# Low parts of the heads' weights: negated copy plus an accumulating DMA in place of a subtraction on VectorE

## The chip, the cores and the metric

The kernel runs on one core of a Trainium2 chip. A core has five engines that run beside each other, each with its own instruction queue that is worked off in order: TensorE (PE, matmuls; its weight loads are PEld), VectorE (DVE), ScalarE (ACT), GpSimd (POOL) and SyncE (SP, which here only issues DMAs). DMAs are issued from SP, ACT or POOL and run on 16 DMA engines. The metric is the device time of one execution in microseconds (us); a smaller one is better.

## The reference, cut to what matters

One decoder layer on a sequence of 512 tokens of width 2048, in float32. The input is normalised and multiplied by one wide matrix `w_in`; its columns feed 8 attention heads of width 128 (the "fox" heads, with a forget gate), 16 recurrent heads of width 64 (RWKV-7), and two gates.

```
h = rmsnorm(x, norm_gain)
u = h @ w_in                                   # 2048 x 12488 weights
u_fox, u_rwkv, g_a, g_b = split(u)
q, k, v, z_a, f = split(u_fox)                 # fox heads
o_a = fox_attention(q, k, v, logsigmoid(f + bias)) * silu(z_a)
r, kr, vr, z_b, w_down, a_down = split(token_shift(u_rwkv))
o_b = groupnorm(rwkv7_scan(r, decay, k, v, kk, b)) ... * silu(z_b)
m = sigmoid(g_a) * (o_a @ w_proj_fox) + sigmoid(g_b) * (o_b @ w_proj_rwkv)
out = rmsnorm(x + m @ w_out, final_norm_gain)
```

## The kernel before, in words

**Numbers as two parts.** TensorE multiplies in a rounded form of float32 (F32R). Each float32 operand is split in a high part (the rounded number) and a low part (what the rounding left), and a product is three matmuls: high x high, high x low, low x high. The normalised input lies in SBUF once as `hhi` and `hlo`. The weights come from HBM piece by piece (`load_raw`, tile `raw_*`), and `split_pieces` makes of each piece `whi_*` and `wlo_*`. From piece 4 on, ACT makes `whi` (L267, a Copy that rounds) and DVE makes `wlo` (L268, raw minus whi). `raw`, `whi` and `wlo` have four buffers each, so a piece takes over the buffers of the piece four before it.

**The heads stage** (about 40 to 930 us) takes 16 units in turn, RWKV pair 0, fox head 0, RWKV pair 1 and so on. Each unit has four tiles of 128 columns of `w_in` (k, r, z, v for an RWKV pair; fq, fk, fv, fz for a fox head), each tile four pieces of 512 weight rows (`HK` = 4 blocks of 128). So there are 64 tiles and 256 pieces of 128x512 (256 KB), and each piece feeds 12 matmuls of 512 columns into `u_*`. In the names `raw_fq_4` is the piece of tile fq that begins at block 4.

Beside the products, as generators that are stepped between matmuls, run the heads' own computations: `rwkv_front` (decay, normalised keys), `rwkv_back` (masked scores `G`, a triangular inverse `W` solved in 31 pairs of DVE instructions, L483 and L643), `rwkv_chain` and `fox_head` (logits, softmax, transposes). `rwkv_chain` goes through 8 chunks of 64 tokens one after the other; in each, PE makes `z`, which DVE and ACT copy to `zt` (L717, L718, half of the partitions each), PE makes `sa`, copied to `AV` (L727, L728), and PE makes `st`, added by DVE into the next state `SV` (L735). The ACT half of `zt` and of `AV` waits for the DVE half of the same tile.

**What sets the order.** PE and SP follow the order of the program text, which a small planner fixes: it counts matmul time in `clock` and resumes each generator after a delay from the table `LAG`. DVE, ACT and POOL are ordered by a scheduler that takes priorities: evictions of products and of the chain have `high_priority(offset=HP)`, HP = 300, the splitting of pieces has HW = 150. On POOL there is little in the heads stage: two elementwise instructions a pair (L533, L483), copies and clears for the chain (L708, L595), and the stores of the heads' results (L774 `ob_d`, L837 `oa_d`).

`next_piece`, called when PE comes to piece i, issues loads up to piece i + 4 and has the split of pieces up to i + 2 put into the program.

After the heads come the gates (from about 930 us; pieces g, then loads named `b` and `X`, where sums of `w_in` blocks are made, one of them by a DMA from POOL that adds into `X`, L985), the projections (p) and the output (o).

Of the kernel before, what the change touches and what calls it, by code (L numbers as in the profile page):

```python
# [9 lines left out]
F32 = mybir.dt.float32  # L10
F32R = mybir.dt.float32r
AF = mybir.ActivationFunctionType
ALU = mybir.AluOpType
# [43 lines left out]
def hybrid_layer(  # L57
# [7 lines left out]
    V, S, G, PE = nc.vector, nc.scalar, nc.gpsimd, nc.tensor  # L65
# [171 lines left out]
    def load_raw(name, srcs, nk, M):  # L237
        raw = wpool.tile([P, nk, M], F32, tag="raw", bufs=RAWS, name=f"raw_{name}")
        for off, src in srcs:
            nc.sync.dma_start(raw[:, :, off:off + src.shape[1]], src.rearrange("(k p) m -> p k m", p=P))  # L240
        return raw

    def next_piece():


        i = used[0]
        used[0] += 1
        while len(raws) < min(i + (RAWS + 1 if i > 3 else 4), len(pieces)):
            raws.append(load_raw(*pieces[len(raws)]))
        split_pieces(i + (3 if i > 3 else 1))  # L250
        got = parts[i]
        parts[i] = None
        return got

    def split_pieces(n):
        while len(parts) < min(n, len(pieces)):
            j = len(parts)
            name, srcs, nk, M = pieces[j]
            raw = raws[j]
            whi = wpool.tile([P, nk, M], F32R, tag="whi", bufs=4, name=f"whi_{name}")  # L260
            wlo = wpool.tile([P, nk, M], F32R, tag="wlo", bufs=4, name=f"wlo_{name}")
            if j < 4:
                G.tensor_copy(whi, raw)
                G.tensor_tensor(wlo, raw, whi.bitcast(F32), ALU.subtract)
            else:
                with tc.high_priority(offset=HW):
                    S.activation(whi, raw, AF.Copy)  # L267
                    V.tensor_tensor(wlo, raw, whi.bitcast(F32), ALU.subtract)  # L268
            parts.append((whi, wlo))


# [7 lines left out]
    def product(ps, name, hi, lo):  # L279

        M, nk = spec[name]
        for k0 in range(0, nk, HK):
            whi, wlo = next_piece()
            for k in range(HK):
                kk = k0 + k
                mm(ps[0:M, :], whi[:, k, :], hi(kk), start=(kk == 0), stop=False)
                yield
                mm(ps[0:M, :], whi[:, k, :], lo(kk), start=False, stop=False)
                yield
                mm(ps[0:M, :], wlo[:, k, :], hi(kk), start=False, stop=(kk == nk - 1))  # L290
                yield
# [52 lines left out]
    for hf in range(2):  # L344
        t = slice(256 * hf, 256 * hf + 256)
        for j in range(0, KC + AHEAD, 2):
            if j < KC:
                turn(hf, j)
            if hf == 0 and j % 4 == 0 and j < KC:
                wd_w.append(next_piece())  # L350
                if j == 0:
                    for tb in range(2, 4):
                        for h2 in range(2):
                            load_x(nc.sync, tb, h2)
                    load_params()
            if hf == 0 and j in (SQ2, SQ3):
                norm_rows(2 if j == SQ2 else 3)
            if j < AHEAD:
                continue
            for kk in range(j - AHEAD, j - AHEAD + 2):  # L360
                whi, wlo = wd_w[kk // 4]
                mm(ps_wd[0:MW, t], whi[:, kk % 4, :], hhi[:, kk, t], start=(kk == 0), stop=False)
                mm(ps_wd[0:MW, t], whi[:, kk % 4, :], hlo[:, kk, t], start=False, stop=False)
                mm(ps_wd[0:MW, t], wlo[:, kk % 4, :], hhi[:, kk, t], start=False, stop=(kk == KC - 1))
            if hf == 1 and j - AHEAD in (4, 8, 12):
                split_pieces(4 + (j - AHEAD) // 4)
# [492 lines left out]
    def stage1():  # L859
# [198 lines left out]
        for g in range(4):  # L1058
            ps = [ps_mm(f"c11_{g}_0"), (ps_mm if g else ps_y)(f"c11_{g}_1")]
            for kb in range(2):  # L1060
                for j in range(4):
                    ws = [next_piece(), next_piece()]
                    order = [(kk, t) for kk in range(2) for t in range(2)]
                    if j == 3:
                        order = [(kk, t) for t in range(2) for kk in range(2)]
                    for kk, t in order:
                        k = 2 * j + kk
                        ah, al = (a[:, KB * kb + k, t * P:(t + 1) * P] for a in (hhi, hlo))
                        whi, wlo = (w[:, 0, :] for w in ws[kk])
                        for a, w, i in ((ah, whi, 0), (ah, wlo, 1), (al, whi, 2)):  # L1070
                            mm(ps[t], a, w, start=kb == 0 and k == 0 and i == 0,
                               stop=kb == 1 and k == KB - 1 and i == 2, skip_group_check=True)
                            yield
                        if j == 3 and kk == 1:
                            if kb == 0:
                                p1 = keep.tile([P, T], F32, tag=KEEP[t], name=f"p1_{g}_{t}")
                                with tc.high_priority(offset=HP):
                                    S.copy(p1, ps[t])
                                    nc.scalar.dma_start(p1_d[g, t], p1)
                            else:  # L1080
                                sg = keep.tile([P, T], F32, tag=KEEP[2 + t], name=f"c11_{g}_{t}")
                                with tc.high_priority(offset=HP):
                                    S.activation(sg, ps[t], AF.Tanh, scale=0.5)
                                store_gate(sg, g, 0, 0, t)
                    if free["fox"] == 7 and first_sums:
                        sum_step(*first_sums.pop(0))
                    if g == 3 and kb == 1 and not first_sums:
                        sum_step("s2", j)
                    if g == 3 and kb == 1 and j == 3:
                        open_late()  # L1090
# [134 lines left out]
    for n in range(4):  # L1225
        pss = four_banks(n, f"o_{n}")
        for kk in range(KC if n < 3 else KC // 2):
            whi, wlo = next_piece()
# [61 lines left out]
```

## Time and profile before

| | |
|---|---|
| median of 3 runs (range) | 1658.53 us (1658.02 to 1660.35) |
| profiled execution: time | 1658.03 us |
| profiled execution: span of its instructions | 1656.3 us |
| PE busy | 1598.2 us, 96% of the span |
| DVE busy | 1125.3 us, 68% |
| ACT busy | 770.0 us, 46% |
| POOL busy | 103.4 us, 6% |
| mean granted TensorE clock | 0.994 of full speed |

Busy shares are means over the whole run. A PE that is busy may still not be at its peak, as matmuls overlap and their ends are modelled; an idle time of PE in the trace is time in which it had nothing to run. "PE sa L136 <- ACT zt L718: 5.1, 8" reads: PE stood idle 5.1 us in 8 places before a matmul into `sa`, until ACT's instruction of line 718 into `zt` was done.

### The profile page before, as it was taken

What the parts mean: (1) busy time and instruction counts of PE and PEld (TensorE: products, weight loads), DVE (VectorE), ACT (ScalarE), POOL (GpSimd) and SP (SyncE); (2) the same over time, 40 slices, a digit from 0 to 9 for tenths busy, and PEclk for the clock granted to TensorE, in tenths of its full rate; (3) what the DMA queues carried; (4) which work ended last, traced back from release to release, by engine and by line L of the source; (5) the groups of instructions that cost most, each with busy time, mean ns of one, the idle gap of its engine ahead of it and who ended that gap; (6) DMA issues with size and microseconds to landing.
All of it is one profiled execution on the core that took longest, in us unless ns stands there. A gap on an engine that the chain in (4) does not pass through costs nothing. (4 is left out here: it accounts for less than half of the span.)

```text
span 1656.3 us, 23493 instructions
## 1 busy us (share of the span) xinstructions
PE 1598.2 (96%) x8378; PEld 1297.9 (78%) x8378; DVE 1125.3 (68%) x2173; ACT 770.0 (46%) x1503; POOL 103.4 (6%) x165
## 2 busy tenths in 40 slices
PE   6999999999999999999999999799999999999998
PEld 6888787787787887878878777578878787888886
DVE  6468777786687687777866869997877335544432
ACT  7533645536436446455364467444444222323322
POOL 3010000000101000001000000011100000001110
PEclk9999999999999999999999999899999999999999
DMA  5443334243333342433333466878775545463422
GB/s 169 99 102 88 86 87 106 64 118 87 87 93 97 88 108 75 105 94 79 97 93 87 124 177 197 267 204 249 209 236 153 178 157 157 149 217 119 140 83 102
DMA packets 238315, 216.39 MB, mean 131 GB/s; under 512 B 40326, under 2 KB 174062, under 8 KB 237558
## 3 DMA queue, kind: packets, MB, share of 16 engines
q1 hardware_dynamic: 224582, 183.40, 39.3%
q0 software_dynamic: 6416, 17.85, 4.7%
q10 hardware_dynamic: 7200, 13.63, 2.2%
q8 instruction: 66, 1.08, 0.3%
q14 instruction: 51, 0.42, 0.1%
HBM read 193.84 MB, written 20.99 MB: 130 GB/s over the span
## 5 line engine op out<-in xcount | busy, mean ns | idle before, releaser
L136 PE MATMUL p<-whi_p,o 128*128 128x512 f32 x512 | 164.7, 398 | 2.2 <-ACT whi_p L267 2.2
L136 PEld LDWEIGHTS p<-whi_p,o 128*128 128x128 f32 x512 | 96.9, 189 | 24.6 <-ACT whi_p L267 3.0
L483 DVE TENSOR_TENSOR Wt<-W,Lt 128x16 f32<-128x16 f32 (+30 forms) x248 | 101.7, 410 | 6.4
L268 DVE TENSOR_TENSOR wlo_p<-raw_p,whi_p 128x512 fp32r<-128x512 f32 x64 | 43.5, 690 | 90.0 <-ACT whi_p L267 90.0
L136 PE MATMUL p<-wlo_p,o 128*128 128x512 f32 x256 | 101.2, 395 | 0.4 <-DVE wlo_p L268 0.4
L267 ACT ACTIVATE whi_p<-raw_p 128x512 fp32r<-128x512 f32 x64 | 40.4, 632 | 121.2 <-DMA raw_p<-in_w_proj_fox_dram 42.7
L268 DVE TENSOR_TENSOR wlo_o<-raw_o,whi_o 128x512 fp32r<-128x512 f32 x56 | 42.4, 761 | 74.9 <-ACT whi_o L267 74.7
L136 PE MATMUL o<-whi_o,mhi 128*128 128x512 f32 x224 | 87.6, 391 | 0.0
L136 PE MATMUL o<-whi_o,mlo 128*128 128x512 f32 x224 | 87.2, 389 | 0.0
L136 PE MATMUL o<-wlo_o,mhi 128*128 128x512 f32 x224 | 87.1, 389 | 0.0
L423 ACT CAST h<-X 128x1024 fp32r<-128x1024 f32 x48 | 50.2, 1052 | 66.9 <-DVE X L483 31.5
L643 DVE TENSOR_REDUCE W<-Wt 128x8 f32<-128x16 f32 (+30 forms) x248 | 72.7, 293 | 5.7
L267 ACT ACTIVATE whi_o<-raw_o 128x512 fp32r<-128x512 f32 x56 | 35.3, 631 | 83.8 <-PE o L136 75.9
L424 DVE TENSOR_TENSOR l<-X,h 128x1024 fp32r<-128x1024 f32 x48 | 58.3, 1222 | 19.2 <-ACT h L423 19.1
L136 PEld LDWEIGHTS p<-wlo_p,o 128*128 128x128 f32 x256 | 48.6, 190 | 11.8 <-DVE wlo_p L268 1.1
L722 ACT ACTIVATE pre<-SV,E 64x64 f32<-64x64 f32 x112 | 38.6, 345 | 39.5 <-DVE SV L735 38.3
L136 PE MATMUL c<-whi_g,hhi 128*128 128x512 f32 x128 | 51.6, 403 | 3.9 <-ACT whi_g L267 2.0
L423 ACT CAST h<-b 128x1024 fp32r<-128x1024 f32 x32 | 33.7, 1054 | 45.4 <-PE y L136 21.1
L136 PE MATMUL c<-wlo_g,hhi 128*128 128x512 f32 x128 | 51.3, 401 | 1.9 <-DVE wlo_g L268 1.9
L136 PE MATMUL u_fq<-hhi,whi_fq 128*128 128x512 f32 x128 | 52.5, 410 | 0.0
L136 PE MATMUL u_fq<-hlo,whi_fq 128*128 128x512 f32 x128 | 52.4, 409 | 0.0
L267 ACT ACTIVATE whi_g<-raw_g 128x512 fp32r<-128x512 f32 x64 | 39.8, 630 | 26.7 <-PE c L136 7.7
(423 smaller groups left out, 4663.9 us busy)
## 6 DMA issues: line engine op xcount, KB each, us to landing
b<-in_w_in_dram SPq DMA_DIRECT2D x64, 512.0 KB
raw_g<-in_w_in_dram SPq DMA_DIRECT2D x64, 256.0 KB
raw_o<-in_w_out_dram SPq DMA_DIRECT2D x56, 256.0 KB
raw_k<-in_w_in_dram SPq DMA_DIRECT2D x32, 256.0 KB
raw_r<-in_w_in_dram SPq DMA_DIRECT2D x32, 256.0 KB
raw_z<-in_w_in_dram SPq DMA_DIRECT2D x32, 256.0 KB
raw_v<-in_w_in_dram SPq DMA_DIRECT2D x32, 256.0 KB
raw_fq<-in_w_in_dram SPq DMA_DIRECT2D x32, 256.0 KB
```

Of the source, the lines that this page charges most:

```text
L136: PE.matmul(out, lhsT=lhsT, rhs=rhs, start=start, stop=stop, **kw)
L267: S.activation(whi, raw, AF.Copy)
L268: V.tensor_tensor(wlo, raw, whi.bitcast(F32), ALU.subtract)
L423: S.copy(hi, a)
L424: V.tensor_tensor(lo, a, hi.bitcast(F32), ALU.subtract)
L483: eng.tensor_tensor(o, a, b, op)
L643: V.tensor_reduce(W[:, :, i], tmp[:, :, 0:i + 1], AX.X, ALU.add)
L722: S.activation(pre[hs[q]], SV[hs[q], c, q, :], AF.Copy, scale=E1[hs[q], c, CH:CH + 1])
```

## The change

In `split_pieces`, pieces whose name begins with k, r, z, v or f (all 256 of the heads; not the first eight of the down projections and none of the gates, projections or output) no longer get their low part from DVE. ACT writes the negated, rounded raw piece into `wlo`, a DMA issued from POOL adds the raw piece onto it (SBUF to SBUF, `accum_op=ALU.add`), and ACT makes `whi` as before. In `next_piece` the splits are put into the program one piece further ahead (i + 4 in place of i + 3) for i from 8 to 249.

```diff
-        split_pieces(i + (3 if i > 3 else 1))
+        split_pieces(i + (4 if 7 < i < 250 else 3 if i > 3 else 1))
...
                 with tc.high_priority(offset=HW):
+                    if name[0] in "krzvf":
+
+                        S.activation(wlo, raw, AF.Copy, scale=-1.0)
+                        G.dma_start(wlo.bitcast(F32), raw, accum_op=ALU.add)
                     S.activation(whi, raw, AF.Copy)
-                    V.tensor_tensor(wlo, raw, whi.bitcast(F32), ALU.subtract)
+                    if name[0] not in "krzvf":
+                        V.tensor_tensor(wlo, raw, whi.bitcast(F32), ALU.subtract)
```

The order of PE and that of SP are the same before and after. On ACT 256 instructions come in, on POOL 256 DMAs, and on DVE 256 go; the scheduler also puts some of DVE's and ACT's other instructions of the heads stage in another order. From about 960 us on, ACT, DVE and POOL run the same rows in the same order.

ACT in the chain of the fourth pair (chunks 3 and 4), before; `zt` and `AV` are the copies that PE waits for, `pre` scales the state for the next chunk, `vT` is the eviction of tile v:

```order
L718 COPY zt_4261<-z_3_4259 64x64
L267 ACTIVATE whi_fq_4_4304<-raw_fq_4_4243 128x512
L728 COPY AV_4017<-sa_3_4274 64x64
L722 ACTIVATE pre_4316<-SV_3271,E_0_483 64x64 x2
L267 ACTIVATE whi_fq_8_4349<-raw_fq_8_4280 128x512
L718 COPY zt_4313<-z_4_4311 64x64
L267 ACTIVATE whi_fq_12_4371<-raw_fq_12_4302 128x512
L728 COPY AV_4017<-sa_4_4331 64x64
```

and after:

```order
L723 COPY zt_4378<-z_3_4376 64x64
L271 ACTIVATE whi_fq_4_4399<-raw_fq_4_4359 128x512
L269 ACTIVATE wlo_fq_4_4400<-raw_fq_4_4359 128x512
L733 COPY AV_4128<-sa_3_4391 64x64
L727 ACTIVATE pre_4435<-SV_3360,E_0_483 64x64 x2
L271 ACTIVATE whi_fq_8_4422<-raw_fq_8_4397 128x512
L269 ACTIVATE wlo_fq_8_4423<-raw_fq_8_4397 128x512
L723 COPY zt_4432<-z_4_4430 64x64
L271 ACTIVATE whi_fq_12_4468<-raw_fq_12_4420 128x512
L733 COPY AV_4128<-sa_4_4450 64x64
```

The same pieces stand at the same places of the chain, with the negating copy (L269) behind the rounding one, ahead of `AV` of chunk 3 and of `zt` of chunk 4.

POOL at the end of the fourth pair's chain, before (`SV` and `AV` belong to the next pair, `ob_d` stores a finished pair):

```order
L837 DMA oa_d<-fz_4345 128x512
L595 MEMSET SV_6698 64x64 x2
L708 COPY AV_6307<-SV_5537 64x8x64 x2
L774 DMA ob_d<-y_5858 128x512
L533 TENSOR_SCALAR a_6431<-a_6431 128x512
```

and after:

```order
L713 COPY AV_5352<-SV_4508 64x8x64 x2
L270 DMA wlo_fv_4_4803<-raw_fv_4_4666 128x512
L270 DMA wlo_fv_8_4840<-raw_fv_8_4800 128x512
L270 DMA wlo_fv_12_4862<-raw_fv_12_4837 128x512
L270 DMA wlo_fz_0_4881<-raw_fz_0_4859 128x512
L270 DMA wlo_fz_4_4900<-raw_fz_4_4878 128x512
L779 DMA ob_d<-y_4820 128x512
L270 DMA wlo_fz_8_4919<-raw_fz_8_4897 128x512
L270 DMA wlo_fz_12_4940<-raw_fz_12_4916 128x512
```

The accumulating DMAs stand in one queue with POOL's other work; the one of `fz_8` is behind the store `ob_d`, which waits for DVE.

## Rows read from the trace of the kernel before

**Rows 1.** Windows: busy us of each engine (instructions), clock, DMA share, GB/s; heads, gates.
```profile
100.00:930.00 830.00, 817.57 (x4771) 662.87 (x4770) 625.58 (x1431) 416.51 (x910) 42.94 (x56) 1.00 0.36 92
1150.00:1200.00 50.00, 50.00 (x220) 41.00 (x220) 41.37 (x41) 22.66 (x26) 3.69 (x4) 1.00 0.80 240
```

**Rows 2.** Windows: seven stretches in which a pair's front and chain begin, the first and the sum.
```profile
170.00:190.00 20.00, 17.20 (x136) 12.73 (x135) 15.58 (x26) 16.00 (x32) 2.38 (x2) 1.00 0.27 66
...
sum 220.00, PE 209.16 PEld 164.72 DVE 151.36 ACT 163.70 POOL 13.31; mean PE 29.88 PEld 23.53 DVE 21.62 ACT 23.39 POOL 1.90
```

**Rows 3.** Waits of PE, 100 to 930 us: us in total, times, longest.
```profile
PE sa L136 <- ACT zt L718: 5.1, 8, 1.5
PE z L136 <- ACT G L693: 1.7, 1, 1.7
PE bt L140 <- ACT BT L668: 1.1, 2, 0.8
```

**Rows 4.** Line 718 (ACT `zt`): what it waited for, who waited for it (us, times).
```profile
  DVE zt L717: 27.6, 31
...
  PEld sa L136: 12.1, 21
  PE sa L136: 5.1, 8
```

**Rows 5.** Waits of DVE, 100 to 930 us: us in total, times, longest.
```profile
DVE AV L727 <- PE sa L136: 16.6, 19, 2.3
DVE zt L717 <- PE z L136: 13.8, 13, 1.6
```

**Rows 6.** Groups of DVE in the same stretch: xcount, busy us, mean ns, idle before.
```profile
L717 DVE COPY zt<-z 64x64 f32<-64x64 f32 x56 | 11.9, 213 | 14.7 <-PE z L136 13.8
L727 DVE COPY AV<-sa 64x64 f32<-64x64 f32 x56 | 11.7, 209 | 16.8 <-PE sa L136 16.6
```

**Rows 7.** Window 100 to 930 us of line 268 alone: DVE busy (instructions).
```profile
100.00:930.00 830.00, 162.84 (x236) 1.00 0.36 92
```

**Rows 8.** Group of ACT, 100 to 930 us, one tile of eight like it.
```profile
L267 ACT ACTIVATE whi_fv<-raw_fv 128x512 fp32r<-128x512 f32 x32 | 20.2, 632 | 28.0 <-PE u_fk L136 27.1 <-DMA Lt<-l_d 0.7
```

**Rows 9.** POOL's queue (packets, MB, share); its DMA issues (count, KB, us to landing).
```profile
q0 software_dynamic: 6416, 17.85, 4.7%
...
X<-in_w_in_dram POOLq DMA_DIRECT2D x16, 512.0 KB, 7.2
...
oa_d<-fz POOLq DMA_DIRECT2D x8, 256.0 KB, 2.3
...
gain<-in_final_norm_gain_dram POOLq DMA_DIRECT2D x1, 1024.0 KB, 5.1
```

**Rows 10.** Timeline (start, us): a tight piece of tile r, twice.
```profile
495.48 0.62 ACT L267 ACTIVATE whi_r<-raw_r 128x512 fp32r<-128x512 f32 x1
...
499.08 0.39 PE L136 MATMUL u_r<-hhi,wlo_r 128*128 128x512 f32 x1
...
719.94 0.61 ACT L267 ACTIVATE whi_r<-raw_r 128x512 fp32r<-128x512 f32 x1
...
723.53 0.39 PE L136 MATMUL u_r<-hhi,wlo_r 128*128 128x512 f32 x1
```

**Rows 11.** Timeline: a low part, and the load that takes its raw buffer.
```profile
475.10 0.68 DVE L268 TENSOR_TENSOR wlo_k<-raw_k,whi_k 128x512 fp32r<-128x512 f32 x1
475.81 0.37 SPq L240 DMA_DIRECT2D raw_r<-in_w_in_dram  x1
```

**Rows 12.** Chain of waits: a raw load of 256 KB; twelve matmuls of 512 columns.
```profile
997.99 3.20 DMA raw_g<-in_w_in_dram
...
1063.42 2.75 PE x L136 x12
```

**Rows 13.** Timeline: a store on POOL, and PE at the piece queued behind it.
```profile
470.50 0.55 POOL L774 DMA_DIRECT2D ob_d<-y  x1 [18.30 <-DVE W L643]
...
476.12 0.39 PE L136 MATMUL u_fz<-hhi,wlo_fz 128*128 128x512 f32 x1
```

## The prediction, made before the changed kernel was run

> **What bounds the kernel now.** I read the windows by stage first. In the heads stage, the only one the change touches, PE is busy 817.6 of 830 us [rows 1], so 12.4 us of idle is all that a faster split can give back there, short of waits that overlapping matmuls hide. DVE is busy 625.6 us (75%) and ACT 416.5 (50%); neither is full on average, but averages hide the stretches. So second: seven stretches in which a pair's front and chain begin, together 220 us, hold 220 - 209.2 = 10.8 us of the 12.4 [rows 2]. There ACT is busy 163.7 us (74%) and DVE 151.4 (69%): ACT is the fuller engine exactly where PE idles. Third, the waits of PE: the largest is `sa` after ACT's `zt`, 5.1 us, and the next ones are ACT's too [rows 3]. Fourth, who was late for `zt`: the line itself shows 5.1 us of idle PE and 12.1 us in which the weight load waited (21 of 56 chunks), part of it under the matmul before; and ACT in turn sat 27.6 us in 31 of 56 chunks until DVE's half was done [rows 4]. DVE waited for PE before its `zt` only 13 times and before `AV` 19 times [rows 5] of 56 each [rows 6]: in the other 43 and 37 it was busy with something else when the product was ready. So the chain queues on both engines, on DVE more often, on ACT where it costs. The weights themselves never show in the waits of PE in this stage.
>
> **The change part by part**, against the profiled execution (1658.0 us, of which 1656.3 are the span; 0.5 us below the median, which is too little to carry).
>
> *DVE loses the subtraction.* Line 268 takes 162.8 us of the 830 [rows 7], 0.69 us each, so a chain copy that becomes ready on DVE meets one 162.8/830 = 20% of the time and then waits half of it, 0.35 us: 112 copies x 0.20 x 0.35 = 7.8 us. Of the `zt` waits only some reach PE (21 of 56 chunks [rows 4]); I take half, **-4 us**. Bounds: 0, if what is next in DVE's queue simply takes the place, and -12.4, all the idle there is.
>
> *ACT gains the negating copy.* 256 of them at the 0.63 us of `whi` [rows 8], the same shape and form; 236 in the 830 us make 149 us, and ACT goes from 50% to 68%. A piece comes each 830/236 = 3.5 us, so the seven stretches get 63 copies, 40 us, and ACT there goes from 74% to 93%. By the same count as for DVE: 112 copies x (0.63/3.5 = 18%) x 0.31 us = 6.3 us, half of it at PE, **+3 us**. In the new order the copy stands right ahead of `AV` or `zt` in several chunks, which is why I don't take less. Bounds: 0, if the scheduler's places fit, and +10, if at 93% a quarter of the 40 us shows.
>
> *POOL's DMA stands between ACT and PE.* Before, a low part was ready 0.7 us after the high one. Now: 0.63 us for the negation and then the DMA from issue to landing. No accumulating copy inside SBUF is in the trace. The nearest rows are POOL's plain 256 KB stores, 2.3 us, and the adding DMA into `X`, 512 KB, 7.2 us [rows 9]. From 2.3 us for 256 KB and 5.1 for 1024 KB a plain transfer has 0.93 us per 256 KB and 1.4 us besides; `X` has (7.2 - 1.4)/2 = 2.9 per 256 KB. That gives 1.4 + 2.9 = 4.3 us, my value, as `X` is the row with the same operation; ends 2.3 and 7.2. So 4.9 us after `whi`. I went through the 256 pieces in the timeline for the time from the end of `whi` to the first matmul with `wlo`: the two tightest have 499.08 - 496.10 and 723.53 - 720.55, 2.98 us each [rows 10], a third 4.2, all of tile r behind the fox softmax on ACT; no other has under 4.9. They fall short by 1.9 + 1.9 + 0.7 = 4.5 us: **+5 us**. At 2.3 us nothing is late (0); at 7.2, 29 pieces are, 42 us summed singly, which is too much as one stall covers the next pieces.
>
> The Trainium skill, "DMA: Bandwidth & Descriptors", section on the anatomy of a DMA on the GpSimd path, gives such a DMA about 2.0 us plus its bytes at 436 GB/s: estimated from that, 2.6 us for 256 KB and 3.2 for 512. The plain stores agree (2.3), `X` at 7.2 does not. By the page this term would be about 0.5 us in place of 5, and the sum 4 us lower.
>
> *The queue on POOL.* The DMA waits for ACT's negation, and behind a waiting instruction of POOL all later pieces wait. The closest place is the store `ob_d`, which waits for DVE: issued at 470.50, done issuing at 471.05, and the piece behind it is wanted at 476.12 [rows 13]: 5.1 us against 4.3. Of seven such places the others read alike but one, which has 2.2 us: **+1 us**; 0 if DVE, relieved, finishes earlier, and 7 x 2.1 = 15 at 7.2 us.
>
> *The loads.* A raw buffer is free when its low part is made: the load goes out 0.03 us after DVE's end [rows 11], now some 4 us later. Ring of four buffers: 0.63 + 0.63 + 4.3 + 3.2 for a raw load [rows 12] = 8.8 us, against four pieces at PE's fastest pace, 4 x 2.75 = 11.0 [rows 12]. Cost 0, with 2.2 us of cover. On SP the small DMAs of the triangular solve stand behind the loads; the planner leaves the solve 42 us, so I cost them at 0; if they were the late ones it would be up to 4 us for each of 8 pairs. DMA share: at queue 0's rate (17.85 MB for 4.7% of the span [rows 9]) the added 67.1 MB take 17.7% of 1656 = 293 us, over 890 us 0.33: from 0.36 to about 0.69. The gates run at 0.80 with no idle PE [rows 1].
>
> *Splits one piece further ahead.* Cost 0: ACT already waits for PE to release the buffers (27.1 us before `whi_fv` alone [rows 8]), so with four buffers they can't run earlier.
>
> Sum: 1658.0 - 4 + 3 + 5 + 1 = **1663 us**, slower by 0.3%. PE's order being fixed, a chain copy that is early gives little, while one that is late stops PE: that asymmetry is the forecast.
>
> **Rivals.**
>
> 1. *DVE was the chain's queue* (faster). For it: DVE kept 43 of 56 `zt` waiting [rows 5, 6] and ACT idled 27.6 us for it [rows 4]; DVE falls to 463 of 830 us, and its softmax and solve come earlier. Against: PE's waits end on ACT [rows 3], and the stretches are ACT's [rows 2]. With the transfer near 2.3 us (no late piece): -8 + 1 + 0 + 0, 1651 us. It decides if DVE's relief reaches PE with all of the 7.8 us.
> 2. *All is hidden* (same). Delays on ACT and relief on DVE cancel and pieces keep their slack, typically some 8 us from `whi` to use: 1658 us. Against it only the tight pieces.
> 3. *The accumulating DMA sets the pace* (much slower). The ring binds when 8.8 us becomes 11.0, at a landing of 6.5 us. `X` speaks for it at 7.2, but with twice the bytes and beside a DMA share of 0.8. At 7.2 each fast piece pays (11.7 - 11.0)/4 = 0.17 us; 110 of the 256 come at the fastest pace, 19 us; at 9 us 0.62 each, 68 us. With late pieces about 1690.
>
> **How the numbers follow.** About 0.2% (3.3 us) is what a measurement tells from no change. The forecast 0.33 (own range 1659 to 1671), rival 1 0.30, rival 2 0.25, rival 3 0.12. Faster is rival 1, 0.30; same is rival 2, 0.25; slower the other two, 0.45. The range reaches down to 1649 (12.4 us of idle would give 1646, never all of it) and up to 1688, with under 0.1 beyond each end. The predicted time is the forecast's 1663.
>
> **What would show it.** In the profile after: line 269 on ACT at 0.63 us x256, ACT near 68% and DVE near 56% of 830 us; the DMA's landing near 4.3 us; waits of PE on DMA `wlo_r` and `wlo_fz` of about 5 us in all, which the profile of before doesn't have; waits of `sa` and `st` on ACT not smaller than before. The forecast is wrong if PE idles less than 12.4 us in the heads stage, if the landing is under 3 us (no late pieces) or above 6.5 (the ring), or if the time changes behind 930 us, where all orders are equal.

## The result, and the profile after

The changed kernel takes **1678.33 us** (median of 4 runs, 1676.83 to 1680.49), the kernel before, run beside it, 1658.36 (1658.02 to 1660.35): a ratio of 1.0117, 95% interval 1.0104 to 1.013. Slower by 1.2%, where 0.3% was forecast. The profiled spans are 1678.8 and 1656.3 us, so the traces have 22.5 us to account for.

Windows of the kernel after, columns as in [rows 1]: the heads, the gates, and four stretches inside the heads in which the granted clock falls.

```profile
100.00:930.00 830.00, 802.91 (x4666) 648.83 (x4665) 476.35 (x1148) 530.01 (x1124) 233.45 (x285) 0.99 0.79 162
1150.00:1200.00 50.00, 50.00 (x220) 41.03 (x219) 40.14 (x40) 23.70 (x27) 4.76 (x4) 1.00 0.76 227
186.60:190.00 3.40, 2.97 (x8) 2.51 (x9) 3.40 (x5) 0.88 (x2) 1.59 (x1) 0.50 0.64 136
282.10:285.50 3.40, 3.40 (x9) 2.32 (x8) 2.15 (x6) 3.01 (x8) 0.85 (x1) 0.51 1.03 232
292.40:295.80 3.40, 3.40 (x12) 2.74 (x11) 0.45 (x3) 2.74 (x7) 0.27 (x2) 0.50 0.45 77
753.20:760.00 6.80, 6.21 (x44) 5.15 (x44) 2.44 (x8) 5.55 (x15) 1.72 (x2) 0.50 0.28 43
```

Against [rows 1], PE idles 830 - 802.9 = 27.1 us in the heads where it idled 12.4, 14.7 us more. ACT went from 416.5 to 530.0 us (64%), DVE from 625.6 to 476.4 (57%), and the DMA share from 0.36 to 0.79. The last four rows are the part that idle time doesn't show: for 17.0 us in all PE was granted 0.50, the level of 1.2 GHz, where the heads stage of before ran at 1.00 throughout. Half of 17.0 is 8.5 us, an estimate of what that costs. 14.7 + 8.5 = 23.2, against 22.5 of the spans. The window holds a little less work after than before, as the gates begin at 954.5 us where they began at 930.8, but between 930 and 954.5 PE doesn't idle. Over the whole span the same comes out: idle time of PE is 1678.8 - 1606.0 = 72.8 us, before 1656.3 - 1598.2 = 58.1, again 14.7 more, and the other 7.8 are busy time. The gates have no idle PE in the window shown, as before.

Waits of PE after, 100 to 930 us (us, times, longest), against [rows 3]:

```profile
PE sa L136 <- ACT zt L723: 9.1, 9, 2.2
PE fl L136 <- ACT BT L673: 3.2, 3, 1.7
PE z L136 <- ACT G L698: 2.7, 1, 2.7
PE fo L136 <- ACT fpT L817: 2.4, 3, 1.1
PE fpt L140 <- ACT fpT L817: 2.4, 1, 2.4
PE fpt L140 <- ACT BT L673: 1.8, 2, 1.4
```

All of these end on ACT. `sa` behind `zt` grew from 5.1 to 9.1 us, and waits of the fox tiles and of the chain's start (`fl`, `fo`, `fpt`), small or absent before, are new. No wait of PE for an accumulating DMA is in the full list either. Line 723 alone (before: [rows 4]): ACT waits less for DVE (16.7 us in 18 chunks, before 27.6 in 31), and PE's weight load waits more for ACT (17.2, 26 times, before 12.1, 21 times).

```profile
  DVE zt L722: 16.7, 18
...
  PEld sa L136: 17.2, 26
```

POOL's queue and its DMA issues after (the kernel before: [rows 9]):

```profile
q0 software_dynamic: 43280, 84.98, 28.7%
...
wlo_k<-raw_k POOLq DMA_DIRECT2D x32, 256.0 KB, 4.5
...
wlo_v<-raw_v POOLq DMA_DIRECT2D x32, 256.0 KB, 3.7
...
ob_d<-y POOLq DMA_DIRECT2D x8, 256.0 KB, 4.0
```

The accumulating DMA lands after 3.7 to 4.5 us (medians by tile; these two rows are the ends), around the 4.3 us that the prediction worked out from `X`, the row with the same operation. Who feels it is SP, as its own waits show, and behind it those that need what SP loads (waits of SP, of ACT and of DVE, 100 to 930 us):

```profile
SPq L240 <- DMA wlo_fq<-raw_fq: 109.0, 28, 7.6
```

```profile
ACT lora_h L428 <- DMA lora<-in_rwkv_a_dram: 16.3, 6, 4.8
...
ACT whi_k L271 <- DMA raw_k<-in_w_in_dram: 8.2, 4, 3.3
...
ACT whi_r L271 <- DMA raw_r<-in_w_in_dram: 5.5, 4, 2.7
```

```profile
DVE A L664 <- DMA W<-w_d: 39.8, 7, 7.0
```

The same rows of the kernel before are small: ACT stood 9.8 us at `lora_h` and 1.9 at raw loads in all (1.4 of them in the row shown), DVE 5.0 at the solve's read-back `W<-w_d`:

```profile
ACT lora_h L423 <- DMA lora<-in_rwkv_a_dram: 9.8, 5, 3.0
...
ACT whi_z L267 <- DMA raw_z<-in_w_in_dram: 1.4, 2, 1.2
```

```profile
DVE A L659 <- DMA W<-w_d: 5.0, 6, 1.9
```

Why the read-back is late stands in the timeline. These are the last row of the third pair's solve on DVE and the four stores of its result (`w_d<-W`) on SP, first before, then after:

```profile
376.99 0.42 DVE L643 TENSOR_REDUCE W<-Wt 128x8 f32<-128x256 f32 x1
377.44 1.72 SPq L647 DMA_DIRECT2D w_d<-W  x4
```

```profile
380.62 0.42 DVE L648 TENSOR_REDUCE W<-Wt 128x8 f32<-128x256 f32 x1
382.61 4.14 SPq L240 DMA_DIRECT2D raw_r<-in_w_in_dram  x2
386.80 2.36 SPq L652 DMA_DIRECT2D w_d<-W  x4
```

Before, SP issues the first store 0.03 us after the solve's end; after, 5.76 us. Two raw loads stand in front of it, and the second waits until 386.33 for an accumulating DMA (`wlo_k`) that holds its buffer. From the second pair to the seventh this delay is 2.6 to 5.8 us, before 0.03 in each. Then the stores and the read-back themselves take longer: SP issues the read-back 1.5 to 3.8 us behind the last store, before 1.2 to 1.3.

One gap, on ACT after (timeline: start, duration, in brackets the idle time before and what ended it). PE idles 1.36 us at 279.2 (`fpt`) and 1.71 us at 281.3 (`fl`), each behind a `BT`; from 282.1 its clock is 0.51.

```profile
276.96 0.63 ACT L269 ACTIVATE wlo_r<-raw_r 128x512 fp32r<-128x512 f32 x1 [1.35 <-DMA raw_r<-in_w_in_dram]
277.50 0.61 ACT L271 ACTIVATE whi_r<-raw_r 128x512 fp32r<-128x512 f32 x1
...
278.63 0.56 ACT L673 COPY BT<-bt 128x512 f32<-128x512 f32 x1
...
279.62 0.63 ACT L269 ACTIVATE wlo_z<-raw_z 128x512 fp32r<-128x512 f32 x1
280.15 0.62 ACT L271 ACTIVATE whi_z<-raw_z 128x512 fp32r<-128x512 f32 x1
280.67 0.57 ACT L673 COPY BT<-bt 128x512 f32<-128x512 f32 x1
```

Both suspects are in this one stretch: ACT stands 1.35 us for a raw load that came late, and in front of each `BT` it makes a negating copy (0.63 us) that the kernel before doesn't have. The trace can't divide the loss between them; the experiments do.

### The profile page after: what moved, and what is told of

It is laid out like the page before. It is cut to its first block, busy times and chain, and to the rows that moved or that the text cites. A ratio compares the mean times of both kernels' runs of the same rounds, so it can differ in the third digit from the quotient of the medians.

```text
span 1678.8 us, 24067 instructions
## 1 busy us (share of the span) xinstructions
PE 1606.0 (96%) x8378; PEld 1302.8 (78%) x8378; DVE 983.1 (59%) x1917; ACT 906.7 (54%) x1759; POOL 317.8 (19%) x421
## 3 DMA queue, kind: packets, MB, share of 16 engines
q0 software_dynamic: 43280, 84.98, 28.7%
## 5 line engine op out<-in xcount | busy, mean ns | idle before, releaser
L990 POOL DMA_DIRECT2D X<-in_w_in_dram x16 | 19.2, 1199 | 190.1 <-DVE l L429 187.7
L136 PE MATMUL u_z<-hlo,whi_z 128*128 128x512 f32 x128 | 52.8, 412 | 0.0
L136 PE MATMUL u_z<-hhi,whi_z 128*128 128x512 f32 x128 | 52.7, 412 | 0.0
```

The costliest lines, as they stand in the source:

```text
L136: PE.matmul(out, lhsT=lhsT, rhs=rhs, start=start, stop=stop, **kw)
L990: G.dma_start(xs[j], rows(g, "21", j), accum_op=ALU.add)
```

## The experiments

All were run beside the kernel before. Times are medians; ratios are to that kernel, with the 95% interval. A difference of two kernels is worked out from their ratios times 1658 us; by the two intervals it is uncertain by 3 to 5 us. The scheduler also puts some of ACT's and DVE's other instructions in another place in each kernel (between experiments 3 and 11, some 70 of about 1050 on ACT and 70 of about 1320 on DVE), and every difference includes that.

**1. The lookahead alone.**

```
-        split_pieces(i + (3 if i > 3 else 1))
+        split_pieces(i + (4 if 7 < i < 250 else 3 if i > 3 else 1))
```

Expected: 

> The kernel before, with only the splits taken one piece further ahead; subtraction on DVE, no accumulating DMA. If the added ACT instruction is the cause of the +20 us (theory A) or the accumulating DMA is (theory D): 1656 to 1660 us, no difference, PE idle 12 to 13 us in the heads stage. If the rounding copy, blocked at ACT's head by an unreleased buffer one piece earlier, is the cause (theory L): 1670 us or more, with zt and fl waits of PE as in the changed kernel.

Measured: 1656.96 us, ratio 0.9992 (0.9976 to 1.0007). Theory L falls; the step "splits one piece further ahead, cost 0" holds. This kernel is the base of experiments 3, 4 and 11.

**2. The negating copy on DVE.**

```
-                        S.activation(wlo, raw, AF.Copy, scale=-1.0)
+                        V.tensor_scalar(wlo, raw, -1.0, None, ALU.mult)
```

Expected: 

> The changed kernel with the negating copy moved from ACT to DVE (a tensor_scalar by -1, some 0.42 us by the nearest row); the accumulating DMA, its traffic, its queue and the lookahead stay. Theory A (ACT is what delays the chain and the fox tiles): 1655 to 1661 us, PE idle 10 to 14 us in the heads stage and no drop of the clock inside it. Theory D (the transfers: share 0.79, landing about 4.3 us, stores and loads slower): 1674 to 1680 us, as changed, with the waits of PE on zt, fl, z, fo as in the changed kernel.

Measured: 1700.06 us, ratio 1.0258 (1.0231 to 1.0285), slower than the change itself, though ACT is down to 400.8 of 830 us and DVE does 0.42 us per piece instead of 0.69. Theory A as the only cause falls. The waits of ACT in this kernel (100 to 930 us) are for late loads, and the DMA's issue stands behind DVE's solve (`W`, `Wt`), as the group of POOL shows (busy, mean ns, idle before and what ended it; the group over 100 to 950 us):

```profile
ACT whi_r L271 <- DMA raw_r<-in_w_in_dram: 30.3, 14, 5.1
ACT lora_h L428 <- DMA lora<-in_rwkv_a_dram: 27.0, 6, 6.4
```

```profile
L270 POOL DMA_DIRECT2D wlo_fz<-raw_fz x28 | 24.3, 867 | 54.3 <-DVE W L648 28.5 <-DVE Wt L488 19.1 <-DVE wlo_fz L269 6.6
```

The time went beyond theory D too (1674 to 1680). That the DMA starts later behind the solve and so frees the raw buffer later fits these rows, but was not tried by itself.

**3. ACT's copy alone, without a DMA.** On top of the lookahead; DVE subtracts as before.

```
                 with tc.high_priority(offset=HW):
+                    if name[0] in "krzvf":
+                        S.activation(wlo, raw, AF.Copy, scale=-1.0)
                     S.activation(whi, raw, AF.Copy)
                     V.tensor_tensor(wlo, raw, whi.bitcast(F32), ALU.subtract)
```

Expected: 

> The kernel before with the lookahead and one more ACT copy per heads piece (the negating copy into wlo, which DVE's subtraction then overwrites): ACT loaded as in the changed kernel, DVE not relieved, no accumulating DMA. Theory A: 1674 to 1686 us (at least the +20, as DVE's subtraction now also waits for it), with drops of the clock in the heads stage. Theory D: 1656 to 1662 us.

Measured: 1673.24 us, ratio 1.0092 (1.0067 to 1.0117), so 1.0092 - 0.9992 = 1.00% or **+16.6 us** for the ACT copy. This is the price of the copy in this kernel, not of ACT's busy time alone: DVE's subtraction overwrites the same `wlo` and so waits for the copy. PE's waits are again ACT's, and the clock falls three times in the heads (3.4 us each at 176.3, 186.5 and 742.9). Waits of PE, 100 to 930 us, and the timeline of ACT ahead of the longest, 2.8 us at `gp` (it begins with 3.68 us in which ACT stands for `lora`, and goes on with two copies of 0.62 us ahead of `BT`):

```profile
PE sa L136 <- ACT zt L720: 4.9, 13, 1.2
PE fl L136 <- ACT BT L670: 4.7, 3, 2.2
PE gp L136 <- ACT BT L670: 3.9, 2, 2.8
```

```profile
739.48 0.40 ACT L425 CAST lora_h<-lora 96x256 fp32r<-96x256 f32 x1 [3.68 <-DMA lora<-in_rwkv_a_dram]
739.79 0.62 ACT L269 ACTIVATE whi_z<-raw_z 128x512 fp32r<-128x512 f32 x1
740.33 0.61 ACT L268 ACTIVATE wlo_z<-raw_z 128x512 fp32r<-128x512 f32 x1
740.85 0.56 ACT L670 COPY BT<-bt 128x512 f32<-128x512 f32 x1
```

**4. DVE's subtraction away, nothing in its place.** On top of the lookahead; PE takes the high part twice.

```
+            if j >= 4 and name[0] in "krzvf":
+                wlo = whi
...
                     S.activation(whi, raw, AF.Copy)
-                    V.tensor_tensor(wlo, raw, whi.bitcast(F32), ALU.subtract)
+                    if name[0] not in "krzvf":
+                        V.tensor_tensor(wlo, raw, whi.bitcast(F32), ALU.subtract)
```

Expected: 

> The kernel before with the lookahead and without the low parts of the heads' weights: PE multiplies by the high part where it took the low one, DVE's 256 subtractions are left out, nothing is put in their place (part of the computation is missing). It gives the DVE term alone. By the prediction's sum 1654 us (-4); by rival 1 1650 us; if DVE is not what PE waits for, 1657 to 1659 us, with the zt waits of PE near 5 us as before.

Measured: 1646.57 us, ratio 0.9929 (0.9908 to 0.9951): **-10.4 us** against the lookahead alone. DVE's relief is worth more than the -4 of the sum; here rival 1 was nearer.

**5. One small load issued earlier, in the changed kernel.** `lora` of the next pair is loaded at the end of the front of this one.

```
         sums[p] = (rhi, rlo)
+        if p + 1 < 8:
+            load_lora(p + 1, w)
```

Expected: 

> The changed kernel with one small load moved: a pair's lora weights (two loads of 48 KB on SP) are issued at the end of the front of the pair before, not at the start of its own, where they stand behind raw loads that wait for the accumulating DMA. Theory Q (in the changed kernel SP's queue makes lora late, ACT stands 16.3 us at lora_h, and three PE gaps of 1.7, 2.4 and 2.2 us with two drops of the clock follow): 1666 to 1672 us, lora_h no longer waiting. Theory A alone (only the added ACT instruction counts): 1676 to 1680 us, the same waits taking the place.

Measured: 1674.97 us, ratio 1.0099 (1.0082 to 1.0116). It doesn't tell: ACT's rounding of `lora` was pulled ahead with the load, so the wait stayed.

```profile
ACT lora_h L428 <- DMA lora<-in_rwkv_a_dram: 14.3, 5, 4.1
```

**6. The accumulating DMA alone.** The low buffer is zeroed on POOL.

```
-                        S.activation(wlo, raw, AF.Copy, scale=-1.0)
+                        G.memset(wlo.bitcast(F32), 0.0)
                         G.dma_start(wlo.bitcast(F32), raw, accum_op=ALU.add)
```

Expected: 

> The changed kernel with the negating copy left out: POOL zeroes the low buffer (a memset of some 0.5 us) ahead of the same accumulating DMA, so the low part is the raw weight (part of the computation is missing). Neither ACT nor DVE has work for the low part; the DMA, its traffic, its queue and the raw ring are those of the changed kernel. Theory A alone: 1645 to 1650 us, as without the subtraction. If the DMA has a price of its own, which by addition is 1678 - (1657 + 16.3 for the ACT copy - 10.4 for the subtraction) = 15 us: 1658 to 1665 us, lora_h waiting on its load and SP on the accumulating DMA.

Measured: 1667.7 us, ratio 1.0049 (1.0024 to 1.0073). Against experiment 4 that is 1.20%, **+19.9 us** for the DMA together with the zeroing (one of the four runs took only 1659.7), where ACT (416.1 of 830 us) and DVE (488.6) have no work for the low part. The zeroing keeps POOL busy, but the solve's rows on DVE are no slower beside it (404 ns, in the changed kernel 410). PE idles 830 - 809.6 = 20.5 us:

```profile
100.00:930.00 830.00, 809.55 (x4725) 658.54 (x4725) 488.61 (x1182) 416.09 (x905) 362.21 (x524) 0.99 0.81 165
```

**7. The negating copy on POOL.**

```
-                        S.activation(wlo, raw, AF.Copy, scale=-1.0)
+                        G.tensor_scalar(wlo, raw, -1.0, None, ALU.mult)
```

Expected: 

> The changed kernel with the negating copy on POOL (a tensor_scalar, 1.47 us by the nearest row, so POOL at (1.47 + 0.87)/3.5 us = two thirds of the heads stage). Theory A alone: 1645 to 1652 us. With the DMA's own price of about 15 us: 1660 to 1668 us. If POOL is too slow for a piece each 2.75 us: above 1675 us, with PE waiting on DMA wlo.

Measured: 1712.64 us, ratio 1.0326 (1.0311 to 1.0342), the third case. The copy takes 1.6 to 1.8 us and POOL is busy 579 of 830 us; PE waits for the DMA's result now, but only 3.0 us for `wlo_fz` and 2.8 for `wlo_k`, and 15.5 us for `zt`. The first instruction of each of the solve's pairs became slower on DVE beside it: 546 ns against 410 in the changed kernel, with the same shapes (the second one, the reduction, takes 294 ns in both). First the group of POOL and of DVE here, then that of the changed kernel:

```profile
L269 POOL TENSOR_SCALAR wlo_k<-raw_k 128x512 fp32r<-128x512 f32 x28 | 50.6, 1807 | 0.3 <-DMA raw_k<-in_w_in_dram 0.3
...
L488 DVE TENSOR_TENSOR Wt<-W,Lt 128x16 f32<-128x16 f32 (+30 forms) x217 | 118.5, 546 | 6.7
```

```profile
L488 DVE TENSOR_TENSOR Wt<-W,Lt 128x16 f32<-128x16 f32 (+30 forms) x219 | 89.7, 410 | 6.7
```

**8. The early load in the kernel before** (the edit of experiment 5).

Expected: 

> The kernel before with the early lora load alone, as a control: ACT waits 9.8 us at lora_h there, but PE's largest waits are elsewhere. Theory Q and A both: 1654 to 1659 us, within 0.2% of before.

Measured: 1652.81 us, ratio 0.9973 (0.9956 to 0.999), a little faster than expected: here `lora_h` waits 4.5 us, not 9.8. It is the fastest complete kernel of the study, by 0.3%.

**9. The ring without the DMA in it.** As 6, but the DMA adds the high part, so that the raw buffer is free when ACT has rounded it.

```
-                        G.dma_start(wlo.bitcast(F32), raw, accum_op=ALU.add)
                     S.activation(whi, raw, AF.Copy)
+                    if name[0] in "krzvf":
+                        G.dma_start(wlo.bitcast(F32), whi.bitcast(F32), accum_op=ALU.add)
```

Expected: 

> As the kernel in which POOL zeroes the low buffer (1667.7 us), but the accumulating DMA reads the high part and not the raw tile (the low part is the high one; part of the computation is missing). The traffic is the same; the raw buffer is free when ACT has rounded it, so that SP's loads wait for ACT again and not for the DMA's landing. Theory R (the DMA's price is the held raw ring: loads, and the small loads behind them on SP, go out some 4 us late): 1645 to 1652 us. Theory T (the price is the traffic itself, share 0.8 against 0.4, which makes small transfers and loads land later): 1662 to 1669 us.

Measured: 1656.6 us, ratio 0.9992 (0.9982 to 1.0001), between the two theories: 0.57% or **9.5 us** below experiment 6, **10.4 us** above experiment 4. The DMA share stays (0.80), SP waits for ACT again:

```profile
100.00:930.00 830.00, 816.00 (x4768) 663.93 (x4767) 497.33 (x1202) 418.53 (x910) 364.37 (x527) 1.00 0.80 167
```

```profile
SPq L240 <- ACT whi_fv L270: 59.8, 26, 4.0
```

SP again issues the solve's first store 0.02 to 0.06 us after the solve (second to seventh pair), while the read-back still follows the last store after 1.7 to 3.4 us. ACT's waits for raw loads fall from 43.8 us in experiment 6 to 4.6; its wait for `lora` stays (17.2 and 18.2).

**10. A plain DMA in its place.** As 6, without zeroing and accumulating.

```
-                        G.memset(wlo.bitcast(F32), 0.0)
-                        G.dma_start(wlo.bitcast(F32), raw, accum_op=ALU.add)
+                        G.dma_start(wlo.bitcast(F32), raw)
```

Expected: 

> As the kernel in which POOL zeroes the low buffer (1667.7 us), but with a plain copying DMA of the raw tile in place of zeroing and accumulating (low part is the raw weight; part of the computation is missing). By the plain stores it lands after 2.3 us and the share of the DMA engines falls to near 0.5. Theories R and T both get cheaper: 1650 to 1658 us. If the price is that of a waiting instruction in POOL's queue or of the issue, which is the same here: 1663 to 1669 us.

Measured: 1648.66 us, ratio 0.9941 (0.9927 to 0.9956), 2 us above no DMA at all, which is within the uncertainty, with the same bytes and as many issues as in experiment 6. So the queue itself and the issue cost next to nothing. What is gone together with the price is the accumulation, in packets, share (0.58) and time to landing, and POOL's zeroing (POOL is busy 164.4 us, in experiment 9 364.4); the zeroing by itself was not tried. The raw buffer waits for the DMA here too, and SP stands for it as long as in experiment 6 (at `wlo_fq` 102.9 us, there 101.3): holding the buffer is dear only with the slower transfer. POOL's queue here, and one issue:

```profile
q0 software_dynamic: 26896, 84.98, 15.7%
wlo_fv<-raw_fv POOLq DMA_DIRECT2D x32, 256.0 KB, 2.7
```

DVE's wait for the solve's read-back goes with the time through experiments 6, 9 and 10 (1667.7, 1656.6, 1648.7 us), one row each:

```profile
DVE A L664 <- DMA W<-w_d: 34.1, 10, 6.1
```

```profile
DVE A L665 <- DMA W<-w_d: 25.4, 8, 5.7
```

```profile
DVE A L663 <- DMA W<-w_d: 18.5, 8, 4.1
```

**11. Half of ACT's copy.** As 3, with 256 of the 512 columns.

```
-                        S.activation(wlo, raw, AF.Copy, scale=-1.0)
+                        S.activation(wlo[:, 0:2, :], raw[:, 0:2, :], AF.Copy, scale=-1.0)
```

Expected: 

> As the kernel with one more ACT copy per piece and no DMA (1673.2 us, +16.3 over the lookahead alone), but the copy takes 256 of the 512 columns, some 0.37 us by ACT's 256-column rows. If ACT's occupied time is what costs: about 60% of 16 us, 1664 to 1669 us. If it is the number of instructions: 1671 to 1675 us. If there is a threshold (ACT at 74% to 93% in the stretches): 1656 to 1661 us.

Measured: 1659.14 us, ratio 0.9998 (0.9983 to 1.0012): 1 us above the lookahead alone, for two thirds of the time per copy (413 ns against 627). ACT is busy 491.8 of 830 us; at 533.5, in experiment 3, it costs 16.6.

```profile
L268 ACT ACTIVATE wlo_fv<-raw_fv 128x256 fp32r<-128x256 f32 x32 | 13.2, 413 | 6.4 <-PE u_fk L136 6.3
```

The price sets in late, or the scheduler places the shorter copy better: some of ACT's and DVE's instructions stand in other places. Which of the two was not tried apart.

**12. The change on every second piece,** with the early load.

```
-                    if name[0] in "krzvf":
+                    if name[0] in "krzvf" and j % 2:
...
-                    if name[0] not in "krzvf":
+                    if not (name[0] in "krzvf" and j % 2):
```

Expected: 

> The kernel before with the early lora load (1652.8 us) and the change on every second heads piece only: 128 pieces with negating copy and accumulating DMA, 128 with DVE's subtraction, lookahead as changed. Halves of the three terms: ACT's busy time as with the half copy (some +1 us there), DVE relieved by half (-5), the accumulating DMA by half (+10 if its price is proportional, about +2 if it also sets in late). Prices with a threshold: 1646 to 1652 us, faster than both kernels. Proportional prices: 1658 to 1665 us.

Measured: 1660.44 us, ratio 1.0014 (1.0 to 1.0029), 7 us slower than experiment 8: the proportional case. Half a dose of the whole isn't free, though half of ACT's copy by itself was.

## Why the prediction was wrong in size

The direction and the landing (4.3 us, measured 3.7 to 4.5) were right, as was one half of the asymmetry behind the forecast: a late copy stops PE. The other half, that an early one gives little, was not: DVE's relief gave 10.4 us. 1678 lies in the range of 1649 to 1688, but the likeliest case ended at 1671, and the direction has luck in it. The two terms that made the sum slower, +5 and +1, cost PE nothing; without them the sum is -1, no change. The time came from other terms.

- **ACT's copy: +3 forecast, +16.6 measured** (experiment 3 against 1), beyond even the upper bound of 10, the uncertainty included. The step that failed is "112 copies x 18% x 0.31 us, half of it at PE": it counted two copies of the chain, `zt` and `AV`, and left out `BT`, `fpT` and `G`, on which most of the added waits end (of the 14.7 us, `zt` has 4.0). In experiment 3 PE's waits for `BT` alone are 9.2 us, in experiment 1 2.4. It also took the delay as an average over the stage, where a copy placed right ahead of a chain's start can cost its whole length, and it had no term for the clock: [rows 1] show it at 1.00, and around gaps of 1.7 to 2.7 us it went to 0.50.
- **The loads: 0 forecast, with 2.2 us of cover.** This step failed too. The cover was worked out for the raw load, landing and rounding alone, as if SP carried nothing else and ACT were always there in time. Of the DMA's 19.9 us, 9.5 went when the raw buffer no longer waited for its landing (experiment 9), and with them the delay of the solve's stores on SP. The sentence on the small DMAs of the solve behind the loads named the place and priced it at 0 by the planner's 42 us; DVE stood 39.8 us at their read-back, at the head of its queue, with its later work behind.
- **The accumulating traffic: not in the sum.** The share was forecast (0.69; it is 0.79) and put aside by the gates' 0.80 without idle. The gates have no solve with small transfers; the heads have, and their read-back still came late in experiment 9, where SP was no longer in the way. That this is the path of the price was not tried apart. Some 8.5 us of the 19.9 separate experiment 9 from 10, in which the transfer is plain and POOL's zeroing is gone.
- **DVE's relief: -4 forecast, -10.4 measured** (experiment 4), the mechanism of rival 1, within the bounds.
- **Late low parts, +5, and POOL's queue, +1: 0.** PE's list of waits after has no accumulating DMA and no store, though the landing is what the estimate assumed. The step that failed is the slack, which was read from the order before. In the new order the two tightest pieces, 2.98 us from the end of `whi` to the first matmul with `wlo`, have 7.9 (503.26 to 511.18 and 731.41 to 739.33); with the lookahead alone they have 3.0.
- **Lookahead: 0, as forecast.**

Taken singly (lookahead, DVE, ACT, DMA), the parts add up to -1.3 - 10.4 + 16.6 + 19.9 = +24.8 us; together they are 1.17%, 19.4 us. The two agree within the uncertainty of the terms. Whether some of the delays overlap is therefore not shown, though the gap at 279 us suggests it: there the late load and the added copies stand on the same engine one behind the other.

Rival 3 had the ring as its mechanism, with landing as the threshold (6.5 us) and PE waiting for low parts as its sign. The ring costs 9.5 us at a landing of 4 us and without that sign: it goes with late raw loads at the head of ACT and with the solve's stores behind the loads on SP.

## What to carry to other kernels

Work that is moved off a full engine is paid where it goes: price the receiving engine by what stands right behind the new instruction, also at places where PE doesn't wait yet, and not by its mean load. A transfer that holds a buffer longer delays the load behind it, and can delay the other transfers in its queue and the engines that wait for them; count those before writing "hidden". Add the clock: here 14.7 us of added gaps came with an estimated 8.5 us more.

## What the runs showed of the hardware

- An accumulating DMA of 256 KB inside SBUF lands after 3.7 to 4.5 us (medians by tile); the plain one of the same tiles after 2.7 (`wlo_fv`) to 3.6 (`wlo_k`). Accumulating, POOL's queue has 43280 packets for 28.7% of the engines' time, plain 26896 for 15.7%, with the same 84.98 MB.
- Beside it, and in the same queue, the store `ob_d` lands after 4.0 us, before after 2.5. The store `oa_d`, also in that queue, hardly changes: 2.4 us, before 2.3.
- Some DVE operations are slower beside POOL's negating copies (experiment 7, POOL busy 70% of the heads): the solve's `Wt` rows, with two inputs in SBUF, take 546 against 410 ns, while its reductions (294) and the copies `zt` (215) stay. Beside POOL's zeroing in experiment 6, with POOL busy 44%, `Wt` takes 404.
- Granted clock: four stretches at 0.50 in the heads, 17.0 us, each in or just behind a gap of PE of 1.7 to 2.7 us. A gap of 2.2 us at 870.7 was not followed by one, so the gap alone doesn't decide. In experiment 3 the clock fell at 176.3, where the longest gap in the 20 us before was 1.0 us.
